# Forgetting attention in a 27,525-instruction transformer kernel: gate rows folded into the score matmul, a bf16 mask, heads in pairs in a fixed order

## The chip, the cores and the metric

The kernel runs on one core of one Trainium2 chip. The metric is the device time of one execution in microseconds (us). The core has five engines that work at the same time, each through its own queue in order: TensorE (PE; its weight loads are listed apart as PEld), VectorE (DVE), ScalarE (ACT), GpSimd (POOL) and SyncE (SP), which here only issues transfers. TensorE's clock is granted at one of two levels; the profile gives it as a share of full speed.

## The reference, cut to what matters

The program computes a mixture-of-experts block and then a block of two layers. Each of these has a token mixer, a cross attention and a feed-forward part. The change lies in the token mixer of the first layer, with 256 tokens, width 1024, 8 heads of 64 and 512 convolution channels:

```python
def forgetting_attention(q, k, v, log_f):
    cum = jnp.cumsum(log_f, axis=1).transpose(0, 2, 1)
    for blk in range(seq // 128):
        lo, hi = blk * 128, (blk + 1) * 128
        s = einsum("bqhd,bkhd->bhqk", q[:, lo:hi], k[:, :hi]) * scale
        s = s + cum[:, :, lo:hi, None] - cum[:, :, None, :hi]
        s = where(causal, s, NEG_INF)
        outs.append(einsum("bhqk,bkhd->bqhd", softmax(s), v[:, :hi]))

def fox_shortconv_mixer(h, w_in, b_f, conv_w, w_out):
    q, k, v, f_logit, b_gate, c_gate, u = split(h @ w_in)
    log_f = log_sigmoid(f_logit + b_f)
    y_a = forgetting_attention(heads(q), heads(k), heads(v), log_f)
    y_b = b_gate * causal_depthwise_conv(c_gate * u, conv_w)
    return concatenate([y_a, y_b]) @ w_out
```

## The kernel before, in words

The program is written as one long trace of operations. A planner puts them in order on each engine: it simulates the engines' time, and on each engine it takes the operation that is earliest in the text among those whose operands and buffers are ready. So work further down fills gaps, and the order in the queues is fixed before the run. `behind(marks)` adds an edge: what is traced in its block goes after the marked operation on the same engine.

Weights come as fp32 tiles through `colw` (256 columns) or `rows_load`, in a ring of three buffers, in the order of the text on SP. `wsp` splits a weight tile into a high part (ScalarE, L76) and the rest (VectorE, L77); a projection multiplies the split parts of weights and activations in three fp32r products (`mm3`, L85 to L87). Most split parts live in a ring of six pairs of buffers; where `wseq` holds an "F", a large buffer with the tag `f8` is used, which attention, recurrence and the prefetch of the next stage share. There are three `f8` buffers. `fgroup` makes one group of 128 output columns: 24 matmuls of 256 columns; `fmaj` makes two groups.

`fox` (L1255) is the token mixer. First come the values projection and the gate (8 rows), then the query and key projections (L1283 to L1285): each `fmaj` leaves two heads below each other in the partitions (0 to 63 and 64 to 127), and one ScalarE operation evacuates it into `qk`. The gate's logarithm and running sum are made on VectorE. `lq` and `rkx` (L1286 to L1302) hold the gate rows: for each head, 40 rows that give cum(query) - cum(key) as a product of their own.

`head` (L1304) does one head. For each of the two query tiles it issues three fp32 matmuls into one bank: query times key (L1310, 64 rows), the gate rows (L1312, 40 rows) and the identity times the causal mask `cm` (L1314). Then come two maxima (L1318, L1319), two exponentials with sums (L1320, L1321), the reciprocal and two scalings (L1322 to L1324), three transposes on TensorE (L1327), the copy into `pt` (L1329) and the products with the values: L1331 for the first key tile, L1332 for the second. The loop over `j` does two heads and one `split` into `ya`.

Behind the heads in the text, the loop of L1347 does the gated convolution in two halves: three projections each (`cproj`, two groups of 128 columns each, into the `acc` banks), the taps on VectorE (L1352 to L1355) and the gate product (L1356), split into `yb`. Last come the four output products with `out_pairs`: 24 matmuls of 512 columns for each of `yb[0]`, `yb[1]`, `ya[0]`, `ya[1]`. In the planned order the convolution groups stand between the steps of the heads. `boundary` then adds to the residual and makes the norm for the next stage. Ahead of `fox`, `first_norms` makes the first norm, with `rs_y` on GpSimd (L1051 to L1054).

Of the kernel before, what the change touches and what calls it, by code (L numbers as in the profile page):

```python
# [45 lines left out]
def block_kernel(ctx: ExitStack, tc: tile.TileContext, io, stop=None, dump=None):  # L46
# [897 lines left out]
    with ExitStack() as pctx:  # L944
# [10 lines left out]
        def wsp(w, a, b):  # L955
            pool = pq
            c = wseq.pop(0) if wseq else "W"
            if c == "F":
                pool = T(p0, [128, 2064], F32R, tag="f8", bufs=3)
            with behind(*marks.get(c, ())):  # L960
                return wsplit(pool, w, a, b, 6)

        def f8():
            return T(p0, [128, 2064], F32, tag="f8", bufs=3)

        def k8(t):
            return t[:, :2048].rearrange("p (a b) -> p a b", a=8)
# [114 lines left out]
                    prenorm_t(t, gn, *hl, rstd2(sx))  # L1082
            return hl

        def fgroup(ps, w, f, hl):
            wH, wL = wsp(w[:, :, f * 128 : (f + 1) * 128], KT, 128)
            po = ps.rearrange("p (t c) -> p t c", t=2)
            for k in range(KT):
                mm3(po, wH[:, k], wL[:, k], hl[0][:, :, k], hl[1][:, :, k], k == 0, k == KT - 1)

        def fmaj(w, hl, tag="sm", ps=None):
            if ps is None:
# [161 lines left out]

        def fox(h, pre):  # L1255
            w = io["ab_w_in_2"][0]
            qk = k8(f8())
            vc = f8()
            vt = vc[:, :1024].rearrange("p (t c) -> p t c", t=2)
            ct = vc[:, 1024:2048].rearrange("p (t c) -> p t c", t=4)  # L1260
# [13 lines left out]
            for k in range(KT):  # L1274
# [5 lines left out]
            G.memset(cm, 0.0)  # L1280
            G.affine_select(out=cm, in_=cm, pattern=[[-1, 128]], compare_op=ALU.is_ge, fill=NEG, base=0,
                            channel_multiplier=1)
            for c in range(2):  # L1283
                A.activation(qk[:, 2 * c : 2 * c + 2], fmaj(colw(w, c * 256), h), AF.Copy, scale=0.125)
                A.copy(qk[:, 4 + 2 * c : 6 + 2 * c], fmaj(colw(w, 512 + c * 256), h))  # L1285
            lq = T(pq, [104, S])  # L1286
            with behind(*marks["B"]):
                V.memset(lq[:64], 0.0)
                V.memset(lq[32:40], 1.0)
                rkx = tok()[:104].rearrange("p (a b) -> p a b", a=4)  # L1290
                V.memset(rkx, 0.0)
                one = wk_()[:8]
                V.memset(one, 1.0)
                oneh = [ident[0:8, b:8:2].unsqueeze(2).to_broadcast([8, 4, S]) for b in range(2)]
                log_sigmoid(pq, fz, fz, 8, S, "wk")
                V.tensor_tensor_scan(lq[0:8], one, fz, 0.0, ALU.mult, ALU.add)
                V.tensor_scalar(fz, lq[0:8], -1.0, None, ALU.mult)
                V.tensor_copy(lq[64:104], lq[0:40])
                for b in range(2):
                    A.copy(rkx[64 * b : 64 * b + 8], oneh[b])  # L1300
                    V.tensor_tensor(rkx[64 * b + 32 : 64 * b + 40], fz.unsqueeze(1).to_broadcast([8, 4, S]), oneh[b],
                                    ALU.mult)  # L1302

            def head(hd, po):  # L1304
                j, b0 = hd // 2, 64 * (hd % 2)
                ps = bank("sm")
                for t in range(2):
                    c0, n = (0, 128) if t == 0 else (128, 256)
                    tq = slice(t * 128, (t + 1) * 128)
                    PE.matmul(ps[:, c0 : c0 + n], qk[b0 : b0 + 64, j, tq], qk[b0 : b0 + 64, 4 + j, 0:n],  # L1310
                              start=True, stop=False)
                    PE.matmul(ps[:, c0 : c0 + n], lq[b0 : b0 + 40, tq], rkx[b0 : b0 + 40, j, 0:n],  # L1312
                              start=False, stop=False)
                    PE.matmul(ps[:, c0 + n - 128 : c0 + n], ident, cm, start=False, stop=True)  # L1314
                mx = T(pq, [128, 2], tag="mx", bufs=4)
                sm = T(pq, [128, 2], tag="smx", bufs=4)
                pr = T(pq, [128, 512], tag="pr", bufs=2)
                V.tensor_reduce(mx[:, 0:1], ps[:, 0:128], axis=AX.X, op=ALU.max, negate=True)  # L1318
                V.tensor_reduce(mx[:, 1:2], ps[:, 128:384], axis=AX.X, op=ALU.max, negate=True)  # L1319
                A.activation(pr[:, 0:128], ps[:, 0:128], AF.Exp, bias=mx[:, 0:1], accum_out=sm[:, 0:1])  # L1320
                A.activation(pr[:, 128:384], ps[:, 128:384], AF.Exp, bias=mx[:, 1:2], accum_out=sm[:, 1:2])  # L1321
                V.reciprocal(sm, sm)  # L1322
                V.tensor_scalar(pr[:, 0:128], pr[:, 0:128], sm[:, 0:1], None, ALU.mult)
                V.tensor_scalar(pr[:, 128:384], pr[:, 128:384], sm[:, 1:2], None, ALU.mult)  # L1324
                pst = bank("sm")
                for i in range(3):
                    PE.transpose(pst[:, i * 128 : (i + 1) * 128], pr[:, i * 128 : (i + 1) * 128], ident)  # L1327
                pt = T(pq, [128, 512], tag="pt", bufs=2)
                V.tensor_copy(pt[:, :384], pst[:, :384])  # L1329
                vs = slice(hd * 64, (hd + 1) * 64)  # L1330
                PE.matmul(po[b0 : b0 + 64, 0:256], vt[:, 0, vs], pt[:, 0:256], start=True, stop=False)  # L1331
                PE.matmul(po[b0 : b0 + 64, 128:256], vt[:, 1, vs], pt[:, 256:384], start=False, stop=True)  # L1332

            ya = [y2(), y2()]
            for j in range(4):
                po = bank("sm")
                head(2 * j, po)
                head(2 * j + 1, po)
                y = ya[j // 2]
                split(po[:, :256], y[0][:, j % 2], y[1][:, j % 2])  # L1340
            V.memset(cu[:, :, 0:2], 0.0)
            yb = []

            def cproj(c0):
                return fmaj(colw(w, c0), h, ps=accb())

            for c in range(2):  # L1347
                fs = slice(c * 2, c * 2 + 2)
                A.copy(ct[:, fs], cproj(2056 + c * 256))
                V.tensor_tensor(cu[:, fs, 2 : S + 2], cproj(2568 + c * 256), ct[:, fs], ALU.mult)  # L1350
                for f in (c * 2, c * 2 + 1):
                    V.tensor_scalar(cv[:, f], cu[:, f, 0:S], pcol("abcw", f), None, ALU.mult)  # L1352
                    for i in (1, 2):
                        V.scalar_tensor_tensor(cv[:, f], cu[:, f, i : i + S], pcol("abcw", i * 4 + f), cv[:, f],
                                               ALU.mult, ALU.add)  # L1355
                V.tensor_tensor(cv[:, fs], cproj(1544 + c * 256), cv[:, fs], ALU.mult)  # L1356
                y = y2()
                A.copy(y[0], cv[:, fs])
                V.tensor_tensor(y[1], cv[:, fs], y[0].bitcast(F32), ALU.subtract)
                yb.append(y)  # L1360
            acc = acc4()
            wo = io["ab_w_out_2"][0]
            out_pairs(acc, wo, [(2, yb[0])], True, False)
            out_pairs(acc, wo, [(3, yb[1])], False, False)
            out_pairs(acc, wo, [(0, ya[0]), (1, ya[1])], False, True)
            return acc

        def lru(h, pre):
# [167 lines left out]
```

## Time and profile before

| | us |
|---|---|
| median of 3 runs | 2400.92 (2395.62 to 2401.7) |
| the profiled execution, whole | 2400.16 |
| its span, first to last instruction | 2398.4 |
| TensorE busy | 2091.6 (87% of the span) |
| VectorE / ScalarE / GpSimd busy | 707.2 / 536.2 / 129.7 |

The first two thirds of the span are the expert layer, where the transfers run at some 400 GB/s. The two-layer block begins at about 1620 us. Its attention stage, from the first scores to the last output product, lies between 1673 and 1770 us. Times in the rows below are from the start of the span. In a timeline, a start is followed by a duration; matmuls are pipelined, so the distance between two starts is what one costs in a row of them. An fp32 matmul shows as two records. "[x <-engine tile line]" is idle time before an instruction and what ended it.

### The profile page before, as it was taken

The numbers are of one execution on the slowest core, as the hardware profiler recorded it, in microseconds if no ns is written. First come the engines' busy times: TensorE is split into PE (matmuls) and PEld (weight loads), VectorE is DVE, ScalarE is ACT, GpSimd is POOL, SyncE is SP. The second block draws the span as 40 slices with busy tenths as digits, with TensorE's granted clock in tenths as the row PEclk, the third lists the DMA queues.
The fourth block names the chain that finished last, engine by engine and source line by source line (L and its number), as shares of the span: only waits on it lengthen the run. The fifth ranks groups of instructions, "written<-read, shape, count | busy, mean of one in ns | idle before, by whom it ended". The sixth has DMA issues, their size and how long they took to land. (4 is left out here: it accounts for less than half of the span.)

```text
span 2398.4 us, 27525 instructions
## 1 busy us (share of the span) xinstructions
PE 2091.6 (87%) x11665; PEld 1258.9 (52%) x11665; DVE 707.2 (29%) x1237; ACT 536.2 (22%) x918; POOL 129.7 (5%) x205
## 2 busy tenths in 40 slices
PE   8998998779879879879877778778999999989998
PEld 7876432224423324423322222227777998977998
DVE  7674011000000000000000000007555545775544
ACT  5533000100000000000000000005354434764442
POOL 1521120000000000000000000002000000000000
PEclk9999999999999999999999999999999999999999
DMA  8327799999999999999999999997333655553653
GB/s 261 91 69 287 296 409 408 407 406 408 405 406 408 405 407 408 405 407 408 405 408 408 407 407 409 407 383 236 113 128 110 205 191 175 170 177 102 210 178 106
DMA packets 267803, 721.56 MB, mean 301 GB/s; under 512 B 7824, under 2 KB 102544, under 8 KB 267680
## 3 DMA queue, kind: packets, MB, share of 16 engines
q1 hardware_dynamic: 267376, 719.65, 79.1%
q8 instruction: 92, 1.51, 0.3%
q14 instruction: 31, 0.25, 0.0%
q10 hardware_dynamic: 304, 0.14, 0.0%
HBM read 718.72 MB, written 1.05 MB: 300 GB/s over the span
## 5 line engine op out<-in xcount | busy, mean ns | idle before, releaser
L768 PE MATMUL mm<-w,t 128*64 128x512 f32 (+3 forms) x1536 | 638.0, 566 | 135.3 <-DMA w<-in_w_up_dram 77.1
L769 PE MATMUL mm<-w,t 128*34 128x512 f32 (+1 forms) x1536 | 636.4, 565 | 0.0
L768 PEld LDWEIGHTS mm<-w,t 128*64 128x64 f32 (+1 forms) x1536 | 200.8, 137 | 324.1 <-issue 120.3
L795 PE MATMUL pj<-w,hT 128*34 128x512 f32 x1376 | 312.4, 597 | 51.7 <-DMA w<-in_w_down_dram 36.3
L779 DVE TENSOR_TENSOR hh<-sl,mm 98x512 f32<-98x512 f32 (+3 forms) x50 | 32.1, 642 | 1098.9 <-PE mm L769 1098.8
L769 PEld LDWEIGHTS mm<-w,t 128*34 128x34 f32 x1536 | 163.8, 113 | 222.7 <-issue 221.9
L77 DVE TENSOR_TENSOR wl<-w,wh 128x1024 fp32r<-128x1024 f32 (+1 forms) x196 | 232.7, 1207 | 159.9 <-ACT wh L76 154.5
L76 ACT CAST wh<-w 128x1024 fp32r<-128x1024 f32 (+1 forms) x196 | 197.5, 1032 | 230.9 <-DMA w<-in_w_ffn_gu_dram 64.4
L795 PEld LDWEIGHTS pj<-w,hT 128*34 128x34 f32 x1376 | 81.3, 112 | 245.8 <-issue 221.9
L776 ACT ACTIVATE sl<-mm 98x512 f32<-98x512 f32 (+3 forms) x50 | 28.0, 560 | 763.2 <-PE mm L769 759.4
L85 PE MATMUL sm<-hH,wh 128*128 128x256 f32 (+1 forms) x520 | 146.7, 282 | 0.0
L87 PE MATMUL sm<-hH,wl 128*128 128x256 f32 (+1 forms) x520 | 146.5, 282 | 0.0
L86 PE MATMUL sm<-hL,wh 128*128 128x256 f32 (+1 forms) x520 | 146.3, 281 | 0.0
L85 PEld LDWEIGHTS sm<-hH,wh 128*128 128x128 f32 (+1 forms) x520 | 97.2, 187 | 0.7
L86 PEld LDWEIGHTS sm<-hL,wh 128*128 128x128 f32 (+1 forms) x520 | 97.2, 187 | 0.7
L87 PEld LDWEIGHTS sm<-hH,wl 128*128 128x128 f32 (+1 forms) x520 | 97.1, 187 | 0.3
L77 DVE TENSOR_TENSOR f<-w,f 128x1024 fp32r<-128x1024 f32 x71 | 84.8, 1220 | 30.4 <-ACT f L76 30.4
L85 PE MATMUL acc<-wh,yH 128*128 128x512 f32 x192 | 78.8, 410 | 5.6 <-ACT yH L1445 4.5
L76 ACT CAST f<-w 128x1024 fp32r<-128x1024 f32 x71 | 72.3, 1047 | 32.6 <-PE acc L87 13.6
L85 PE MATMUL pj<-uyH,wh 128*128 128x272 f32 x256 | 77.2, 303 | 1.2 <-ACT qT L314 1.2
L86 PE MATMUL acc<-wl,yH 128*128 128x512 f32 x192 | 78.1, 407 | 0.0
L87 PE MATMUL pj<-uyH,wl 128*128 128x272 f32 x256 | 75.7, 296 | 0.0
(468 smaller groups left out, 2974.9 us busy)
## 6 DMA issues: line engine op xcount, KB each, us to landing
w<-in_w_gate_dram SPq DMA_DIRECT2D x64, 2048.0 KB, 23.6
w<-in_w_up_dram SPq DMA_DIRECT2D x64, 2048.0 KB, 23.9
w<-in_w_down_dram SPq DMA_DIRECT2D x64, 2048.0 KB, 24.0
w<-in_w_down_dram SPq DMA_DIRECT2D x30, 1536.0 KB, 18.9
w<-in_w_ffn_gu_dram SPq DMA_DIRECT2D x44, 1024.0 KB, 5.6
w<-in_w_gate_dram SPq DMA_DIRECT2D x16, 1920.0 KB, 24.0
w<-in_w_up_dram SPq DMA_DIRECT2D x16, 1920.0 KB, 19.9
w<-in_w_ffn_down_dram SPq DMA_DIRECT2D x22, 1024.0 KB, 6.1
```

The source lines that it names most:

```text
L76: A.copy(hv, w)
L77: V.tensor_tensor(lv, w, hv.bitcast(F32), ALU.subtract)
L85: PE.matmul(ps, lh, rh, start=first, stop=False)
L86: PE.matmul(ps, lh, rl, start=False, stop=False)
L87: return PE.matmul(ps, ll, rh, start=False, stop=last)
L768: PE.matmul(ps[:m, :hw], xs[:, k, e * CAP : e * CAP + m], w[k][:, :hw], start=st, stop=sp)
L769: PE.matmul(ps[64 : 64 + CAP, :hw], xs[:, k, es], w[k][:, hw:], start=st, stop=sp)
L776: A.activation(sl[r, :hw], pg[r, :hw], AF.Silu)
L779: V.tensor_tensor(hh[r, :hw], sl[r, :hw], pu[r, :hw], ALU.mult)
L795: PE.matmul(dn[64 * c : 64 * c + CAP], hT_[:, j * CAP : (j + 1) * CAP], d[j][:, c * 512 : (c + 1) * 512], start=f == 0, stop=f == DFF // 1 ...
```

## The change

Query rows (0 to 63), gate rows (64 to 71 and 96 to 103) and zero rows between them stand in one tile for all heads, `qh`, and the same for keys, `kh`; both are `f8` buffers. A head's score of one query tile is then one matmul over 104 rows. The constant rows are filled on GpSimd, as is a one-hot pattern that picks each head's gate row. The evacuation of the projections is by half the partitions (four ScalarE operations for the queries, two on ScalarE and two on VectorE for the keys). The mask is put into the bank first, by one bf16 matmul of 384 columns (`idb`, `cmb`). The `f8` ring has four buffers in place of three.

`head` is taken apart into `scores`, `soft`, `turn` and `values`, and the convolution into twelve `pieces`, each one group of 128 columns. The loop over pairs issues them in a fixed order: scores of two heads, two pieces, transposes of two heads, one piece, values of two heads. `mk` holds the last TensorE instruction of each step, and the next step goes behind it. The value products of the two heads alternate. The output products come in the order `yb[0]`, `ya[0]`, then `yb[1]` and `ya[1]` together.

```diff
-                pool = T(p0, [128, 2064], F32R, tag="f8", bufs=3)
+                pool = T(p0, [128, 2064], F32R, tag="f8", bufs=4)
...
-            return T(p0, [128, 2064], F32, tag="f8", bufs=3)
+            return T(p0, [128, 2064], F32, tag="f8", bufs=4)
...
-            qk = k8(f8())
+            qh, kh = k8(f8()), k8(f8())
...
+            cmb, idb = T(pq, [128, 384], BF16), T(pq, [128, 128], BF16)
+            G.memset(cmb, 0.0)
+            G.tensor_copy(cmb[:, 0:128], cm)
+            G.tensor_copy(cmb[:, 256:384], cm)
+            G.tensor_copy(idb, ident)
+            oneh = ident[0:8, 0:8].unsqueeze(2).to_broadcast([8, 8, S])
+            G.memset(qh[64:96], 0.0)
+            G.memset(qh[96:104], 1.0)
+            G.memset(kh[64:104], 0.0)
+            G.tensor_copy(kh[64:72], oneh)
             for c in range(2):
-                A.activation(qk[:, 2 * c : 2 * c + 2], fmaj(colw(w, c * 256), h), AF.Copy, scale=0.125)
-                A.copy(qk[:, 4 + 2 * c : 6 + 2 * c], fmaj(colw(w, 512 + c * 256), h))
+                pq_ = fmaj(colw(w, c * 256), h)
+                for b in range(2):
+                    A.activation(qh[0:64, 4 * c + b : 4 * c + 4 : 2], pq_[64 * b : 64 * b + 64], AF.Copy, scale=0.125)
+                pk_ = fmaj(colw(w, 512 + c * 256), h)
+                A.copy(kh[0:64, 4 * c : 4 * c + 4 : 2], pk_[0:64])
+                last = V.tensor_copy(kh[0:64, 4 * c + 1 : 4 * c + 4 : 2], pk_[64:128])
...
-                V.tensor_copy(lq[64:104], lq[0:40])
-                for b in range(2):
-                    A.copy(rkx[64 * b : 64 * b + 8], oneh[b])
-                    V.tensor_tensor(rkx[64 * b + 32 : 64 * b + 40], fz.unsqueeze(1).to_broadcast([8, 4, S]), oneh[b],
-                                    ALU.mult)
+                for c in range(2):
+                    hs = slice(4 * c, 4 * c + 4)
+                    A.copy(qh[64:72, hs], fc.unsqueeze(1).to_broadcast([8, 4, S]))
+                    V.tensor_tensor(kh[96:104, hs], fz.unsqueeze(1).to_broadcast([8, 4, S]), oneh[:, hs], ALU.mult)
...
+            def cproj(c0, use):
+                wt, ps = colw(w, c0), accb()
+                for f in range(2):
+                    def piece(f=f):
+                        sp = wsp(wt[:, :, f * 128 : (f + 1) * 128], KT, 128)
+                        with behind(*mk):
+                            m = fgroup(ps[:, f * 256 : (f + 1) * 256], wt, f, h, sp)
+                        mk[:] = [m]
+                        if f:
+                            use(two(ps))
+                    pieces.append(piece)
...
+            def scores(hd):
                 ps = bank("sm")
-                for t in range(2):
-                    c0, n = (0, 128) if t == 0 else (128, 256)
-                    tq = slice(t * 128, (t + 1) * 128)
-                    PE.matmul(ps[:, c0 : c0 + n], qk[b0 : b0 + 64, j, tq], qk[b0 : b0 + 64, 4 + j, 0:n],
-                              start=True, stop=False)
-                    PE.matmul(ps[:, c0 : c0 + n], lq[b0 : b0 + 40, tq], rkx[b0 : b0 + 40, j, 0:n],
-                              start=False, stop=False)
-                    PE.matmul(ps[:, c0 + n - 128 : c0 + n], ident, cm, start=False, stop=True)
+                with behind(*mk):
+                    PE.matmul(ps[:, :384], idb, cmb, start=True, stop=False)
+                    for t, c0, n in ((0, 0, 128), (1, 128, 256)):
+                        m = PE.matmul(ps[:, c0 : c0 + n], qh[0:104, hd, t * 128 : (t + 1) * 128], kh[0:104, hd, 0:n],
+                                      start=False, stop=t == 1)
+                mk[:] = [m]
+                return ps
...
+            def values(j, pts):
                 po = bank("sm")
-                head(2 * j, po)
-                head(2 * j + 1, po)
+                with behind(*mk):
+                    for t, (o, i0, i1) in enumerate(((0, 0, 256), (128, 256, 384))):
+                        for b in range(2):
+                            vs = slice((2 * j + b) * 64, (2 * j + b + 1) * 64)
+                            m = PE.matmul(po[64 * b : 64 * b + 64, o:256], vt[:, t, vs], pts[b][:, i0:i1],
+                                          start=t == 0, stop=t == 1)
+                mk[:] = [m]
...
+            for j in range(4):
+                pss = [scores(2 * j + b) for b in range(2)]
+                prs = [soft(ps) for ps in pss]
+                for i in range(2):
+                    pieces.pop(0)()
+                pts = [turn(pr) for pr in prs]
+                pieces.pop(0)()
+                values(j, pts)
             acc = acc4()
             wo = io["ab_w_out_2"][0]
             out_pairs(acc, wo, [(2, yb[0])], True, False)
-            out_pairs(acc, wo, [(3, yb[1])], False, False)
-            out_pairs(acc, wo, [(0, ya[0]), (1, ya[1])], False, True)
+            out_pairs(acc, wo, [(0, ya[0])], False, False)
+            out_pairs(acc, wo, [(3, yb[1]), (1, ya[1])], False, True)
```

## Rows read from the trace of the kernel before

**Rows 1.** Stretches: length; busy PE, PEld, DVE, ACT, POOL; PE clock; DMA share, GB/s.

```profile
1676.00:1726.70 50.70, 50.03 (x365) 44.52 (x363) 29.40 (x59) 18.55 (x36) 0.00 (x0) 1.00 0.39 125
1726.70:1744.00 17.30, 13.82 (x46) 9.21 (x47) 7.72 (x18) 4.30 (x13) 0.00 (x0) 0.71 0.18 61
1744.00:1770.00 26.00, 25.50 (x112) 19.13 (x111) 11.12 (x17) 9.83 (x20) 1.43 (x4) 1.00 0.37 122
```

**Rows 2.** The same for TensorE alone: length, busy, clock, DMA share, GB/s.

```profile
1732.90:1744.10 11.20, 10.30 (x30) 0.54 0.00 0
```

**Rows 3.** TensorE's waits, 1673 to 1770: us in total, times, longest.

```profile
PE sm L1327 <- DVE pr L1323: 2.3, 1, 2.3
PE sm L1331 <- DVE pt L1329: 1.7, 2, 0.9
```

**Rows 4.** Timeline of TensorE: one head's values, the next head's scores, split products.

```profile
1706.79 0.65 PE L1331 MATMUL sm<-pt,f 128*64 128x256 f32 x2
1707.27 0.38 PE L1332 MATMUL sm<-pt,f 128*64 128x128 f32 x2
1707.58 0.49 PE L1310 MATMUL sm<-f 64*128 64x128 f32 x2
1707.91 0.38 PE L1312 MATMUL sm<-tok,t 40*128 40x128 f32 x2
1708.22 0.49 PE L1314 MATMUL sm<-t,t 128*128 128x128 f32 x2
1708.64 0.70 PE L1310 MATMUL sm<-f 64*128 64x256 f32 x2
1709.17 0.59 PE L1312 MATMUL sm<-tok,t 40*128 40x256 f32 x2
1709.70 0.49 PE L1314 MATMUL sm<-t,t 128*128 128x128 f32 x2
1709.94 0.36 PE L86 MATMUL acc<-hL,wh 128*128 128x256 f32 x1
1710.14 0.29 PE L87 MATMUL acc<-hH,wl 128*128 128x256 f32 x1
1710.26 0.28 PE L85 MATMUL acc<-hH,wh 128*128 128x256 f32 x1
```

**Rows 5.** Timeline of TensorE in the expert layer: products for two halves of the partitions.

```profile
1524.26 0.49 PE L768 MATMUL mm<-w,t 128*64 128x384 f32 x1
1524.27 0.49 PE L769 MATMUL mm<-w,t 128*34 128x384 f32 x1
1524.58 0.49 PE L768 MATMUL mm<-w,t 128*64 128x384 f32 x1
```

**Rows 6.** Timeline of VectorE: first reduction and last scaling of two heads.

```profile
1710.22 0.29 DVE L1318 TENSOR_REDUCE mx<-sm 128x1 f32<-128x128 f32 x1 [1.21 <-PE sm L1314]
...
1712.29 0.35 DVE L1324 TENSOR_SCALAR pr<-pr,smx 128x256 f32<-128x256 f32 x1
...
1718.23 0.29 DVE L1318 TENSOR_REDUCE mx<-sm 128x1 f32<-128x128 f32 x1 [1.75 <-PE sm L1314]
...
1723.63 0.34 DVE L1324 TENSOR_SCALAR pr<-pr,smx 128x256 f32<-128x256 f32 x1
```

**Rows 7.** GpSimd, groups by line and form: a fill (busy us, mean ns).

```profile
L833 POOL MEMSET ysb<- 128x1024 f32 x2 | 1.8, 952 | 39.3 <-PE mm L707 39.3
```

**Rows 8.** ScalarE, groups by line and form, 1615 to 1770: query evacuation.

```profile
L1284 ACT ACTIVATE f<-sm 128x512 f32<-128x512 f32 x2 | 1.2, 589 | 0.0
```

**Rows 9.** Timelines: end of the gate rows, first scores, last output product.

```profile
1667.65 2.46 DVE L1301 TENSOR_TENSOR tok<-t,t 8x1024 f32<-8x1024 f32 x2
...
1673.09 0.49 PE L1310 MATMUL sm<-f 64*128 64x128 f32 x2
...
1769.58 0.40 PE L87 MATMUL acc<-wh,yL 128*128 128x512 f32 x1
```

## What the change does to the time: the prediction, made before the run

> **What bounds the kernel now.** I read the stretches first: they tell which engine sets the pace of the attention stage and where it loses it. From 1676 to 1726.7 us TensorE is busy 50.03 of 50.70 us at a granted clock of 1.00, while VectorE is busy 29.4 and ScalarE 18.6: the stage is bound by TensorE, and whatever is taken out of its queue there ends the stage earlier. Between 1726.7 and 1744 us it is busy only 13.82 of 17.30 at a mean clock of 0.71, and from 1744 on it is full again [rows 1]. So there is a hole 17 us long. Its second part, 1732.9 to 1744.1, runs at 0.54, which is mostly the lower of the two levels, 1.2 GHz [rows 2]. The list of TensorE's waits names what opened it: the transposes of L1327 wait for the normalised rows of L1323 (2.3 us, once) and the value products of L1331 for the copy of L1329 (1.7 us in two) [rows 3]. That is one head's chain from scores to softmax to transposes to values with nothing left to put beside it: by 1726 all twelve convolution groups have been used as filler, and the last three heads run almost alone. Last I read the timeline of one head for the price of each matmul [rows 4].
>
> **Scores, on the path.** A head now issues six fp32 matmuls: L1310, L1312 and L1314 for each of the two query tiles. From the first (1707.58) to the first matmul of other work (1709.94) that is 2.36 us [rows 4]. The starts in between show the parts: the 128-column ones are 0.31 to 0.42 apart, the 256-column ones 0.53. After the change a head has three: one bf16 matmul of 384 columns with the mask, and the two score products with 104 rows, which hold query, key and gate rows together. The row count does not show in the price: 64 rows (1708.64 to 1709.17) and 40 rows (1709.17 to 1709.70) both take 0.53 for 256 columns, so I take 0.33 and 0.53 for the new ones. No bf16 matmul stands in this trace. Nearest is the split product with fp32r operands, 256 columns in 0.12 us (1710.14 to 1710.26) [rows 4], which makes 0.18 for 384. The other end is the fp32 rate: 128 more columns cost 0.53 - 0.33 = 0.20, so 384 cost about 0.75. I take 0.24, near the fp32r row because bf16 is no wider than fp32r, with a little for the change of operands. New sum 0.24 + 0.33 + 0.53 = 1.10; saved 2.36 - 1.10 = 1.26 per head, 8 x 1.26 = 10.1 us. Ends: 6.0 (mask at 0.75) and 11.7 (mask 0.18, and products at 0.72 together because the switches between 40 and 128 rows are gone).
>
> **Values, on the path.** Each head issues L1331 and L1332, 0.48 + 0.31 = 0.79 us [rows 4]. The number of instructions stays, but the order changes: for each key tile the products of head 2j go to partitions 0 to 63 and those of head 2j+1 to 64 to 127, one right behind the other. The expert layer does just this in L768 and L769: two products for different halves of the partitions start 0.01 us apart, and the next pair stands 0.32 behind for 384 columns of one pass [rows 5]; they run side by side. So a pair should take 0.79 in place of 1.58: 4 x 0.79 = 3.2 us. Ends: 0 and 3.2. The Trainium skill says the same in "TensorE: Matmul & The Clock Gate", Part 3 (packing small matmuls): outputs that start in different column groups run concurrently. By that rule the sum below stands; without it, it would be 3.2 us smaller.
>
> **The hole, on the path.** The new order lays two convolution groups between a pair's scores and its transposes, and a third between transposes and values; `mk` chains them on TensorE. Twelve groups, three per pair, so the last pair has its fillers too. Then the two waits, 4.0 us [rows 3], go, and with them the low clock: 10.30 us of work at 0.54 would take 10.30 x 0.54 = 5.6 us at full clock, which gives back 4.7 [rows 2]. Together 8.7. What is late next: behind the last values stand the output products of `yb[0]` and `ya[0]`, whose operands are long ready, so the split of `ya[1]` and the gate product of `yb[1]` lie beside them.
>
> **What the fixed order costs.** A chained TensorE can no longer take other convolution work when a softmax is late. The cover is two groups of 24 matmuls, 48 x 0.12 = 5.8 us. From the first reduction to the end of the normalisation a head needs 2.4 us where VectorE is free (1710.22 to 1712.64), and 5.7 where weight splits and convolution taps stand between (1718.23 to 1723.97) [rows 6]. So the second head of a pair is ready 0.3 + 2.4 to 0.3 + 5.7 us after its scores, against 5.8. Behind the transposes there is one group, 2.9 us, for two copies. I take 0.5 us a pair, 2 in all; ends 0 and 10 (2.5 a pair, when two slow softmaxes meet on one VectorE). Queued behind a waiting transpose are the third group, the values and the next scores: the whole chain waits.
>
> **What lies beside other work.** GpSimd gets three fills and one copy of 2048 columns and four small operations: at 0.95 us for 1024 columns [rows 7] some 1.9 each, about 8 us, and under 2 for the small ones. Ahead of the gate rows it has all of the first projections; its cover is gone only if the fills are queued in front of the `rs_y` operations of the first norm, on which the first transposes wait: 0 to 1.9 us (one fill), and I take 0. ScalarE gets two more evacuations of 0.59 (L1284) [rows 8], VectorE two of about that and loses four fills and a copy. Both have slack in the query and key projections, where TensorE runs without a gap. The gate rows: the products of L1301 end at 1670.1 and the first scores start at 1673.09 [rows 9], 3 us of slack; the two ScalarE copies, so far made early, now follow the scan, but only the first is needed for the first four heads. No load moves: the order of the transfers on SP stays, and the heads issue none. The fourth `f8` buffer shifts the pool behind it by 8 KB, so other transfers wait for other buffers of the expert layer, and later weight splits find one more free buffer. The trace shows no price; I bound it by the longest single TensorE wait of the stage, 2.3 us [rows 3], to either side, and take 1 us of loss.
>
> **Sum.** 10.1 + 3.2 + 8.7 - 2 - 1 = 19.0 us. The profiled execution took 2400.16 us, of which the span is 2398.4; 2400.16 - 19.0 = 2381.2. The median of the runs is 0.8 above that execution, so 2382.
>
> **Rivals.** (a) The hole stays, at another place: the last values, their split and the output weights come too late, or the planner lets the filler run out. For it speaks that this happened to the kernel before; against it the fixed count of fillers. Only scores and values are gained: 13.3 - 1 to 3; time about 2390. (b) Slower: the softmax of a pair does not fit under its two groups, since VectorE takes splits and convolution taps first, and TensorE idles in each of the four pairs long enough to lose its clock. Its price per pair is that of the old hole, 4.0 idle, and 4.7 of low clock, 35 in all; less the 22 gained (10.1 + 3.2 + 8.7) the kernel ends at about 2414. It decides from 5.5 us a pair. For it speaks the 5.7 us softmax, against it that all four pairs must then be as slow, and that a wait of 0.3 to 2.5 us is shorter than the two that cost the clock here, 4.0 together. The Trainium skill, in "TensorE: Matmul & The Clock Gate" (Why this matters for your kernels), warns of idle gaps between bursts of matmuls because the clock falls to half; rows 2 agree, 0.54 behind the waits. (c) The new forms do not pay: the mask at the fp32 rate, values one behind the other, stalls of 2.5 us a pair. 6.0 + 0 + 8.7 - 10 - 1 = 3.7 us; 2397, within the noise. (d) More than forecast: no stalls, all the upper ends, and the spare buffer helps later stages: 11.7 + 3.2 + 8.7 + 2.3 = 25.9; 2375 or below.
>
> **How the numbers follow.** Forecast (2376 to 2388) 0.57; (a) 0.19; (b) 0.09; (c) 0.09; (d) 0.06. A measurement of this kernel can tell about 0.3%, 7 us, from no change. Faster by more: forecast, (a), (d) and a small part of (c), 0.83; within 0.3%: most of (c), 0.08; slower: (b), 0.09. The range leaves out (b) and the far ends of (c) and (d): 2375 to 2397.
>
> **What would show it.** Right: between the end of the key projection and the boundary TensorE at clock 1.00 with under 3 us idle; from a head's mask matmul to its last score about 1.1 us; value products of two heads starting within 0.02 us of each other; the stage ending near 1750 in place of 1770 [rows 9]. Wrong: waits of the transposes for the normalised rows in each pair, a stretch at 0.5, bf16 matmuls of 0.6 us or more, or a first norm that waits for GpSimd.

## The result, and the profile after

The changed kernel takes 2368.89 us (median of 4 runs, 2362.77 to 2369.3); the kernel before took 2398.36 in the same comparison (4 runs, 2395.62 to 2401.7). The ratio is 0.9864, with a 95% interval of 0.985 to 0.9877: faster, by 29 us, which is 13 us below the forecast of 2382 and below its range. The profiled execution took 2369.3 us (span 2367.5), 30.9 less than the 2400.16 of the profiled execution before. All sums below are between these two executions.

First the stretches of the attention stage of the changed kernel: length, busy time of PE, PEld, DVE, ACT and POOL with instruction counts, granted TensorE clock, DMA share, GB/s.

```profile
1673.00:1700.00 27.00, 27.00 (x221) 25.52 (x220) 22.86 (x50) 13.93 (x33) 0.00 (x0) 1.00 0.52 164
1700.00:1727.00 27.00, 27.00 (x195) 23.90 (x194) 19.72 (x38) 13.45 (x26) 0.00 (x0) 1.00 0.47 163
1727.00:1744.00 17.00, 16.41 (x73) 12.93 (x71) 9.93 (x11) 8.26 (x17) 1.93 (x5) 1.00 0.49 165
```

TensorE is busy in every microsecond but the last 0.6, at a clock of 1.00. The hole of [rows 1] and the 0.54 of [rows 2] are gone. TensorE's waits from 1660 to 1760 (total, times, longest) hold nothing of the stage any more; what is left belongs to the boundary behind it:

```profile
PE acc L1106 <- DVE hL L82: 0.9, 2, 0.5
PE sm L1025 <- DVE tok L1021: 0.6, 1, 0.6
```

The two waits of [rows 3] have no successor. Now TensorE's timeline around one pair's scores, around the first pair's values, and at the end of the stage (start, duration, engine, line, tiles, shapes):

```profile
1672.88 0.34 PE L1349 MATMUL sm<-t,t 128*128 128x384 bf16 x1
1673.05 0.82 PE L1351 MATMUL sm<-f,f 104*128 104x128 f32 x4
1673.71 0.33 PE L1349 MATMUL sm<-t,t 128*128 128x384 bf16 x1
1673.87 0.82 PE L1351 MATMUL sm<-f,f 104*128 104x128 f32 x4
1674.34 0.47 PE L85 MATMUL acc<-hH,wh 128*128 128x256 f32 x1
...
1683.75 0.87 PE L1385 MATMUL sm<-pt,f 128*64 128x256 f32 x8
1684.56 0.34 PE L1349 MATMUL sm<-t,t 128*128 128x384 bf16 x1
...
1742.55 0.40 PE L87 MATMUL acc<-wh,yL 128*128 128x512 f32 x1
1743.54 0.44 PE L1025 MATMUL sm<-t,tok 128*128 128x128 f32 x2 [0.58 <-DVE tok L1021]
```

The first head of the pair, with the second behind it, takes 1673.71 - 1672.88 = 0.83 us from mask to mask. The second, with a convolution group behind it, takes 1674.34 - 1673.71 = 0.63: there the next matmul's start comes 0.2 us sooner. Over all eight heads it is 5.85 / 8 = 0.73, where [rows 4] show 2.36. A pair's values take 1684.56 - 1683.75 = 0.81, where one head alone took 0.79. The first scores start as before, at 1672.88 against 1673.09 in [rows 9], and the stage ends 27 us sooner, at 1742.78 in place of 1769.81.

I counted each matmul from its own start to the start of the next, waits taken out, from the first score to the last output product:

| us | before | after | difference |
|---|---|---|---|
| scores | 20.87 | 5.85 | -15.0 |
| transposes of the softmax | 4.12 | 2.13 | -2.0 |
| values | 7.11 | 3.79 | -3.3 |
| convolution groups | 35.63 | 35.26 | -0.4 |
| output products | 24.52 | 22.87 | -1.65 |
| waits | 4.47 | 0.0 | -4.5 |
| stage | 96.72 | 69.90 | -26.8 |

The other 4.1 us lie outside. The two feed-forward stages take 192.68 and 191.83 in place of 195.20 and 194.23, -4.9 together; the stretches ahead of the scores and behind the output products are 1.6 shorter; the expert layer ends 0.7 later (in the profiles of this study its end moves between 1625 and 1633); and the recurrent stage is 1.9 longer. For the last of these TensorE's waits in that stage give the place (before from 2036 to 2132, after from 2005 to 2103). Before:

```profile
PE sm L1025 <- DVE tok L1021: 0.7, 1, 0.7
```

After:

```profile
PE sm L1025 <- DVE tok L1021: 2.4, 1, 2.4
```

The boundary's transposes wait 2.4 us for the normalised tokens in place of 0.7. ScalarE's timeline shows what came in between. Before, the sum of squares of the new residual (L1003) starts as soon as VectorE has it:

```profile
2126.29 0.63 ACT L1003 ACTIVATE junk<-hx 128x512 bf16<-128x512 f32 x1 [1.92 <-DVE hx L1076]
```

After, the split of an output weight of the cross attention into an `f8` buffer stands ahead of it in ScalarE's queue, and waits for its transfer:

```profile
2097.03 1.05 ACT L76 CAST f<-w 128x1024 fp32r<-128x1024 f32 x1 [2.62 <-DMA w<-in_w_xo_dram]
2097.98 0.63 ACT L1003 ACTIVATE junk<-hx 128x512 bf16<-128x512 f32 x1
```

From the start of L1076 to that of L1003 it is 2.49 us (2095.49 to 2097.98) in place of 0.84 (2125.45 to 2126.29). The kernel before makes this split only behind the boundary (2144.56); the kernel with the fourth buffer alone, below, has it in the same place as here, where it waits 1.18 us. So the spare buffer brings the split forward, and what that costs depends on when its transfer lands.

### The profile page after: what moved, and what is told of

Read it like the earlier page. It is cut to its first block, busy times and chain, and to the rows that moved or that the text cites. A ratio compares the mean times of both kernels' runs of the same rounds, so it can differ in the third digit from the quotient of the medians.

```text
span 2367.5 us, 27434 instructions
## 1 busy us (share of the span) xinstructions
PE 2065.2 (87%) x11609; PEld 1240.0 (52%) x11609; DVE 709.1 (30%) x1235; ACT 538.9 (23%) x920; POOL 139.2 (6%) x213
## 5 line engine op out<-in xcount | busy, mean ns | idle before, releaser
L77 DVE TENSOR_TENSOR wl<-w,wh 128x1024 fp32r<-128x1024 f32 (+1 forms) x196 | 234.8, 1216 | 137.2 <-ACT wh L76 130.8
L86 PE MATMUL sm<-hL,wh 128*128 128x256 f32 (+1 forms) x520 | 144.6, 278 | 0.0
L77 DVE TENSOR_TENSOR f<-w,f 128x1024 fp32r<-128x1024 f32 x71 | 85.7, 1222 | 48.7 <-ACT f L76 48.7
L86 PEld LDWEIGHTS sm<-hL,wh 128*128 128x128 f32 (+1 forms) x520 | 96.8, 186 | 0.7
L86 PE MATMUL acc<-wl,yH 128*128 128x512 f32 x192 | 77.1, 401 | 0.0
```

The source lines that it names most:

```text
L77: V.tensor_tensor(lv, w, hv.bitcast(F32), ALU.subtract)
L86: PE.matmul(ps, lh, rl, start=False, stop=False)
```

## The experiments

**The fourth buffer alone.** The kernel before with four `f8` buffers and nothing else:

```
-                pool = T(p0, [128, 2064], F32R, tag="f8", bufs=3)
+                pool = T(p0, [128, 2064], F32R, tag="f8", bufs=4)
...
-            return T(p0, [128, 2064], F32, tag="f8", bufs=3)
+            return T(p0, [128, 2064], F32, tag="f8", bufs=4)
```

> The kernel before, with four f8 buffers in place of three and nothing else changed. Theory 1: the spare buffer is what shortened the two feed-forward stages of the changed kernel (195.2 to 192.7 us and 200.5 to 198.1 us); then those two stages lose about 2.5 us each here too, the attention stage stays at 96.7 us with its hole, and the kernel is about 3 to 5 us faster (2396 against 2400). Rival: those 5 us come from another order that the planner found once the attention stage had changed; then this kernel is within 1 us of before and both feed-forward stages are as before.

Measured: 2394.87 us, ratio 0.9978 (0.9967 to 0.9988), 5 us faster. The attention stage is as it was (96.18). The feed-forward stages take 192.84 and 191.69, as in the changed kernel. In the first of them TensorE's waits before were these:

```profile
...
PE sm L1025 <- DVE tok L1021: 1.0, 2, 0.6
PE acc L86 <- DVE f L77: 0.9, 1, 0.9
...
```

and with four buffers these:

```profile
PE acc L1105 <- ACT hH L81: 1.5, 1, 1.5
PE sm L1025 <- DVE tok L1021: 1.0, 2, 0.6
...
```

The wait for a weight split held in an `f8` buffer (`f`, L77) has gone. It explains 0.9 of the 2.4 us. Most of the rest is no listed wait but spread over the stage: its 960 split products of 256 columns take 112.9 us from start to start in place of 114.1. Why is open. The gain belongs to the buffer and not to the attention stage.

**The new form in the old order of text, without the chain.** The heads have the mask, the 104-row products and their tiles as in the change; the text goes from one head's scores through its softmax to its transposes, then to the next head and the pair's values, the convolution groups follow all heads, the output products have their old order, and `mk` stays empty:

```
-                pss = [scores(2 * j + b) for b in range(2)]
-                prs = [soft(ps) for ps in pss]
-                for i in range(2):
-                    pieces.pop(0)()
-                pts = [turn(pr) for pr in prs]
-                pieces.pop(0)()
+                pts = [turn(soft(scores(2 * j + b))) for b in range(2)]
                 values(j, pts)
+            while pieces:
+                pieces.pop(0)()
```

> The changed kernel with the new score form, but in the order of the kernel before: no chain on TensorE, heads one after the other in the text, convolution groups behind them, output products in the old order. Theory 1: the form alone gives what the scores measured, 8 x (2.36 - 0.73) = 13.0 us, and 3.3 us at the values, while the hole at the end of the heads stays with some 4.5 us of waits and as much of low clock; the attention stage takes about 80 us and the kernel about 2380. Rival: once the scores are short, more of a head's time is softmax, the planner uses up its filler at the same point, and the hole grows by what the scores gave: stage 85 us or more, kernel 2385 or more.

Measured: 2370.86 us, ratio 0.9885 (0.9867 to 0.9904); the stage takes 74.16. Scores 5.46, values 5.55, waits 1.83. Both expectations missed, for the planner filled nearly all of the hole by itself. What is left of the waits is this pair of lines in TensorE's timeline (idle time before the instruction and its releaser in brackets):

```profile
1714.18 0.86 PE L1382 MATMUL sm<-pt,f 128*64 128x256 f32 x6 [1.54 <-DVE pt L1373]
1715.34 0.30 PE L1371 MATMUL sm<-t,pr 128*128 128x128 f32 x1 [0.29 <-DVE pr L1363]
```

So the form alone takes 22.0 of the 26.3 us by which the changed kernel's stage is shorter than that with four buffers (96.18).

**The order alone.** The fixed order and the chain of the change, with a head's six old score matmuls:

```
+            def scores(hd):
+                ps = bank("sm")
+                with behind(*mk):
+                    j, b0 = hd // 2, 64 * (hd % 2)
+                    for t in range(2):
...
+                        PE.matmul(ps[:, c0 : c0 + n], lq[b0 : b0 + 40, tq], rkx[b0 : b0 + 40, j, 0:n],
+                                  start=False, stop=False)
+                        m = PE.matmul(ps[:, c0 + n - 128 : c0 + n], ident, cm, start=False, stop=True)
+                mk[:] = [m]
```

> The changed kernel with its fixed order, value order and four buffers, but with the old scores: six fp32 matmuls a head, gate rows and fp32 mask as products of their own. Theory 1: the hole is gone and the scores cost 2.36 us a head again: attention stage 69.9 + 8 x 1.63 = 83 us, no waits, kernel about 2382. Rival: part of the 15 us that the score lines lost was low clock and not form; then the scores here take less than 2.2 us a head and the kernel is at 2378 or below.

Measured: 2381.68 us, ratio 0.9932 (0.9915 to 0.9948); stage 89.47, waits 0.0, values 3.76. The stage is 6 us longer than the 83 of the first theory, and the surprise is why. TensorE alone, one microsecond a row (length, busy with count, granted clock, DMA share, GB/s), from the first pair of scores, which begins at 1667.98:

```profile
1668.00:1669.00 1.00, 1.00 (x7) 1.00 0.55 62
...
1670.00:1671.00 1.00, 1.00 (x7) 1.00 1.09 389
1671.00:1672.00 1.00, 1.00 (x5) 0.68 1.10 362
1672.00:1673.00 1.00, 1.00 (x3) 0.50 1.01 314
...
1677.00:1678.00 1.00, 1.00 (x7) 0.50 0.00 0
1678.00:1679.00 1.00, 1.00 (x10) 0.90 0.00 0
1679.00:1680.00 1.00, 1.00 (x11) 1.00 0.00 0
```

and its timeline over the fall:

```profile
1667.98 0.49 PE L1346 MATMUL sm<-f 64*128 64x128 f32 x2
...
1669.04 0.70 PE L1346 MATMUL sm<-f 64*128 64x256 f32 x2
1669.57 0.59 PE L1348 MATMUL sm<-tok,t 40*128 40x256 f32 x2
...
1671.71 1.22 PE L1346 MATMUL sm<-f 64*128 64x256 f32 x2
1672.73 1.05 PE L1348 MATMUL sm<-tok,t 40*128 40x256 f32 x2
```

TensorE has work in every row and waits for nothing, and still the clock goes to 0.50, the 1.2 GHz level, 3 us after the old scores of two heads began. The same matmul of 256 columns takes 0.53 to its successor at 1669.04 and 1.02 at 1671.71. The clock returns at 1678 to 1679, among convolution groups. The clock falls again with the third and the fourth pair, and not with the second. Transfers don't decide it: none runs where the last of these falls comes (the last two figures of the row), and a kernel below keeps 1.00 beside busier queues.

```profile
1722.00:1723.00 1.00, 1.00 (x6) 0.78 0.00 0
```

Over all three falls the scores take 21.27 in place of 8 x 2.36 = 18.9, and the convolution groups 39.35 in place of 35.26: together the 6 us. So a pair of old scores in one go can lower the clock without a wait; it did so in three pairs of four.

**The row count.** The changed kernel, its 104-row products each as 96 rows and the 8 rows of the key gates:

```
-                        m = PE.matmul(ps[:, c0 : c0 + n], qh[0:104, hd, t * 128 : (t + 1) * 128], kh[0:104, hd, 0:n],
-                                      start=False, stop=t == 1)
+                        for r in (slice(0, 96), slice(96, 104)):
+                            m = PE.matmul(ps[:, c0 : c0 + n], qh[r, hd, t * 128 : (t + 1) * 128], kh[r, hd, 0:n],
+                                          start=False, stop=t == 1 and r.stop == 104)
```

> The changed kernel with each 104-row score product taken apart into one of 96 rows and one of 8 rows (partitions 96 to 103), same result. Theory 1: a switch between whole-array products and products on a few partitions costs time of its own, which is why the old scores cost 2.36 us and not the 1.1 + 0.8 us that columns alone explain; then a head's scores go from 0.73 us to more than 1.38, by 0.1 us or more for each of four switches: about 1.8 us a head, 8 to 9 us in all. Rival: only columns count: 0.73 + 0.22 + 0.43 = 1.38 us a head, 5.2 us in all.

Measured: 2381.78 us, ratio 0.9935 (0.9917 to 0.9954); scores 17.25, so 2.16 a head in place of 0.73. The first head's timeline:

```profile
1673.97 0.34 PE L1349 MATMUL sm<-t,t 128*128 128x384 bf16 x1
1674.14 2.05 PE L1352 MATMUL sm<-f,f 96*128 96x128 f32 x8
1676.13 0.34 PE L1349 MATMUL sm<-t,t 128*128 128x384 bf16 x1
```

and the weight loads beside it (the bracket is time in which the loads waited for nothing that the profile names):

```profile
1673.97 1.20 PEld L1352 LDWEIGHTS sm<-f,f 96*128 96x128 f32 x6
1675.50 0.29 PEld L1352 LDWEIGHTS sm<-f,f 8*128 8x128 f32 x2 [0.33 <-issue]
1676.12 0.10 PEld L1349 LDWEIGHTS <-t 128*128 128x128 bf16 x1 [0.33 <-issue]
```

Two more products a head, of 128 and 256 columns, should add 0.65 us by their columns (the whole 0.66 of L1351 above). They add 1.43. The other 0.78 go with the four changes between the whole array and 8 rows, about 0.2 each, and at two of them the loads stand still for 0.33. The Trainium skill, in "TensorEngine Tiling (Array Packing)", Key Properties, says that a change of the tiling mode drains TensorE. The pauses agree with that; no run shows in which mode the 8-row products ran.

**Count and width without the small rows.** As many fp32 products as the old heads had and as wide, but all on 104 or 128 rows: each score product twice, and the mask in fp32 for each query tile. The doubled product makes the scores twice as large, so its output is another:

```
-                    PE.matmul(ps[:, :384], idb, cmb, start=True, stop=False)
...
+                        for i in range(2):
+                            PE.matmul(ps[:, c0 : c0 + n], qh[0:104, hd, t * 128 : (t + 1) * 128], kh[0:104, hd, 0:n],
+                                      start=i == 0, stop=False)
+                        m = PE.matmul(ps[:, c0 + n - 128 : c0 + n], ident, cm, start=False, stop=True)
```

> The changed kernel with as many and as wide score products as the old form, six fp32 products a head, but all over the whole array: each 104-row product is issued twice (so the scores come out doubled, which changes the result) and the mask is one fp32 product of 128 columns for each query tile. Theory 1: the old form's price above its columns, and its low clock, came from products on 64 and 40 rows and the switches to and from them; then a head costs its columns alone, 4 x 0.22 + 2 x 0.44 = 1.76 us, 3.5 us a pair, the granted clock stays at 1.00 through the heads, and the stage takes 69.9 + 8 x 1.03 = 78 us. Rival: six fp32 products in a row are dear in any shape and let the clock fall; then a head takes 2.2 us or more, a stretch behind a pair shows a clock under 1.00, and the stage takes 85 us or more.

Measured: 2375.49 us (one run); stage 77.77, scores 14.04, 1.76 a head. One head, from 1673.24 to 1675.00:

```profile
1673.24 0.61 PE L1351 MATMUL sm<-f,f 104*128 104x128 f32 x4
1673.68 0.39 PE L1353 MATMUL sm<-t,t 128*128 128x128 f32 x2
1673.91 1.03 PE L1351 MATMUL sm<-f,f 104*128 104x256 f32 x4
1674.77 0.39 PE L1353 MATMUL sm<-t,t 128*128 128x128 f32 x2
1675.00 0.61 PE L1351 MATMUL sm<-f,f 104*128 104x128 f32 x4
```

A product of 128 columns costs 0.22 and one of 256 costs 0.43. TensorE over a stretch with these scores:

```profile
1660.00:1680.00 20.00, 20.00 (x171) 1.00 0.71 215
```

The clock holds, here and in the three stretches of 20 us behind it. With the same number and width, two things are missing: the 0.6 us a head (2.36 - 1.76) and the fall of the clock. Both belong to the products on 64 and 40 rows with their changes. In the kernel with 96 and 8 rows, which has four such changes a head, the clock falls once, behind the third pair, again with no wait of TensorE in the stage:

```profile
1708.00:1711.00 3.00, 3.00 (x16) 0.50 0.23 93
```

So products on 64 and 40 rows aren't needed for it. Which of the two, few rows or the changes, lowers the clock isn't settled.

**The mask in fp32.** The changed kernel with `cmb` and `idb` in fp32:

```
-            cmb, idb = T(pq, [128, 384], BF16), T(pq, [128, 128], BF16)
+            cmb, idb = T(pq, [128, 384]), T(pq, [128, 128])
```

> The changed kernel with the mask product of 384 columns in fp32 in place of bf16. Theory 1: fp32 costs by columns, two records of 384 columns, 0.64 us for 0.17, so 0.5 us more a head, 4 us in all (stage 74 us), and no fall of the clock, because the product covers the whole array like its neighbours. Rival: the old scores were dear because they were fp32 and came in a row of six, and their long runs alone let the clock fall; then here, too, a stretch shows a granted clock under 1.00 and the stage is over 76 us.

Measured: stage 74.11, scores 9.98 in place of 5.85. The kernel's 2369.05 us (one run) say little, because its expert layer ended 4 us earlier.

```profile
1669.98 0.81 PE L1349 MATMUL sm<-t,t 128*128 128x384 f32 x2
1670.63 0.82 PE L1351 MATMUL sm<-f,f 104*128 104x128 f32 x4
```

The mask costs 0.65 in fp32 and 0.17 in bf16 (1672.88 to 1673.05 above): 4.1 us for eight heads, and the clock stays. This is the price of the type alone, as expected.

**Values head by head.** The changed kernel with the two loops of `values` exchanged:

```
-                    for t, (o, i0, i1) in enumerate(((0, 0, 256), (128, 256, 384))):
-                        for b in range(2):
+                    for b in range(2):
+                        for t, (o, i0, i1) in enumerate(((0, 0, 256), (128, 256, 384))):
```

> The changed kernel with the value products of a pair one head after the other, as before, in place of alternating. Theory 1: alternating products for the two halves of the partitions run side by side and that is all the gain at the values: 0.8 us a pair becomes 1.6, stage 69.9 + 3.2 = 73.1 us. Rival: the gain came from making the two heads' products in one go, without a switch to other work in between; then the pair stays under 1.2 us and the stage under 71.5.

Measured: 2368.87 us (one run), stage 70.03, values 4.03 in place of 3.79.

```profile
1682.81 0.88 PE L1385 MATMUL sm<-pt,f 128*64 128x256 f32 x8
1683.62 0.34 PE L1349 MATMUL sm<-t,t 128*128 128x384 bf16 x1
```

Still 0.81 for a pair. Products for the two halves of the partitions run side by side in either order, as long as both heads' stand together in the queue. Where they stood apart, in the kernel with the form alone and the one without the chain, the sum was 5.5.

**Without the chain.** The changed kernel with the four lines `mk[:] = [m]` taken out, so that the planner orders TensorE's work:

> The changed kernel without the chain on TensorE: text order of pairs and groups as in the change, but the planner may take other work. Theory 1: with short scores the planner fills nearly as well by itself: stage 70 to 72 us, waits under 1 us, kernel within 0.2% of the changed one. Rival: the chain is what keeps fillers for the last pair; then waits of 2 us or more come back near the end of the heads and the stage is 74 us or more, as in the form alone (74.2).

Measured: 2368.58 us, ratio 0.9873 (0.9856 to 0.989), no other than with the chain. The stage takes 72.23, 2.3 more (values 5.49, scores 6.44), waits 0.0. What the chain holds together is worth 2.3 us of the stage, which can't be told apart in the kernel's time.

**Without the groups between.** The chain kept, but the three convolution groups of a pair behind its values:

```
-                for i in range(2):
-                    pieces.pop(0)()
                 pts = [turn(pr) for pr in prs]
-                pieces.pop(0)()
                 values(j, pts)
+                for i in range(3):
+                    pieces.pop(0)()
```

> The changed kernel with no convolution group between a pair's scores and its transposes nor between transposes and values; the three groups follow the values. The chain holds, so TensorE must wait for each softmax. Theory 1: four waits of 3.5 to 5 us for the softmax and four of about 1 us for the copies, 18 to 24 us in all, stage 88 to 94 us at a clock that stays at 1.00, because each wait stands alone between three groups. Rival (the prediction's slower case): each wait takes the clock down with it, some 4.7 us more a pair, stage over 100 us and the kernel at 2400 or above.

Measured: 2389.43 us, ratio 0.9953 (0.9938 to 0.9969); stage 91.67. TensorE waits 11.9 us in eight waits, which are two for each pair:

```profile
1672.41 0.61 PE L1373 MATMUL sm<-t,pr 128*128 128x128 f32 x3 [3.00 <-DVE pr L1365]
1673.55 0.61 PE L1373 MATMUL sm<-t,pr 128*128 128x128 f32 x3 [0.53 <-DVE pr L1365]
```

and its clock falls in every stretch that holds a pair:

```profile
1660.00:1680.00 20.00, 16.45 (x118) 0.91 0.51 158
1680.00:1700.00 20.00, 17.31 (x124) 0.91 0.16 53
```

The two stretches behind these show 0.91 as well: one fall for each pair. Of the 21.8 us over the changed kernel 11.9 are waits. At 0.91 over 20 us the lower clock takes 1.8 us a pair at most, some 7 of the other 9.9. The rest isn't clock: the transposes cost 4.99 in place of 2.13, and the first pair's stand ahead of its fall; a product with a wait behind it is counted to its end and not to the next start. So with the new form the clock falls behind waits, and a pair without cover costs 5.4 us. The first theory's stage of 88 to 94 us was met; its 18 to 24 us of waits and its clock of 1.00 were not.

**A fifth buffer.** Since the fourth helped, a fifth, paid for by one pair of the buffers for weight splits (6 to 5):

```
-                pool = T(p0, [128, 2064], F32R, tag="f8", bufs=4)
+                pool = T(p0, [128, 2064], F32R, tag="f8", bufs=5)
...
-                return wsplit(pool, w, a, b, 6)
+                return wsplit(pool, w, a, b, 5)
```

> The changed kernel with a fifth f8 buffer, paid for with one of the six pairs of small split buffers. Theory 1: the fourth buffer took away the waits of the feed-forward stages' first products for late splits, and a fifth finds nothing more to take; within 0.2% of the changed kernel, feed-forward stages 192 to 193 us. Rival: more large buffers let the next stage's weights come still earlier, and each feed-forward stage loses another microsecond or more.

Measured: 2377.31 us, ratio 0.9915 (0.9894 to 0.9935), slower than the change. The feed-forward stages are at 195.63 and 194.11 again and the second cross stage at 70.77 (68.07). Two things changed at once, so whether the missing pair or the fifth buffer itself costs the time isn't shown; together they lose the gain of the fourth, which neither theory had. No kernel tried is faster than the change by more than a measurement tells.

## Why the prediction was right or wrong

The prediction had 19.0 us, the two executions differ by 30.9. Its mechanism held: TensorE bounds the stage, what leaves its queue comes off the end, and the hole closes. The direction is right, and inside the stage every gain came; the cost of the fixed order did not. The missing 11.9 us are 5.1 outside the stage and 6.8 inside, by the steps:

**The spare buffer: wrong sign, the first step that failed.** I took 1 us of loss, because "the trace shows no price", and named a gain only in rival (d). The buffer brings 5 us, shown by the kernel that has nothing else. [rows 3] were the wrong rows to bound it by: they are of the attention stage, and the place to look was the list of waits of the stages that draw on `f8`, where `PE acc L86 <- DVE f L77` stood in both feed-forward stages. Even that row, 0.9 us each, would have given 1.8 of the 4.9. A loss came too, in the recurrent stage: the split brought forward by the buffer makes the boundary's transposes wait 1.7 us longer. Outside the stage the forecast was +1 and the outcome -4.1.

**Scores: mis-sized, the second step that failed.** Forecast 1.10 a head, measured 0.73: 3.0 us for eight. The mask came at 0.17 instead of 0.24, the end of the range that goes by the fp32r rate of [rows 4]. The products together cost 0.66 instead of 0.86; the last 0.1 is the sooner start of the group behind every second head. What failed is "the row count does not show in the price": in [rows 4] each of the first five start-to-start distances, from which I took my prices, held a change of rows as well. Against 0.22 and 0.43 for products that follow others of the whole array, the old distances are 0.33, 0.31, 0.42, 0.53 and 0.53: each change cost 0.1 to 0.2, 0.6 a head. I had put this into the upper end (0.72 together), where the trace already spoke for it: the 0.24 of the last L1314 before the split products was a 128-column product without a change behind it, beside 0.42 for the same line with one.

**Values: right size, other reason.** 3.3 us against 3.2. The new order within a pair isn't what makes them run side by side; that the two heads' products are neighbours is.

**The hole: right in sum, its cause half told.** The waits went (4.5 against 4.0). One reading was off: only two of the last three heads ran almost alone, the last head's scores stand among the output products, at 1748.26. The table's remaining gains, which are 2.0 of the scores beyond 8 x (2.36 - 0.73) = 13.0, and 2.0, 1.65 and 0.4 on transposes, output products and convolution, make 6.0, where I had 4.7 for the low clock. [rows 1] bound the clock's part: 17.30 x (1 - 0.71) = 5.0 us at most; the rest isn't parted. I named the waits as the cause of the 0.54 in [rows 2]. The experiments show a fall from either: behind waits with the new form (0.91 over 20 us), and in the old scores without any wait (0.50). Which did it before can't be told, since there both came together. The rule that I cited from the Trainium skill, "TensorE: Matmul & The Clock Gate" (Why this matters for your kernels), that idle gaps between bursts of matmuls lower the clock, agrees with the kernel without groups; the kernel with the order alone goes beyond it, since its clock fell with no gap.

**The fixed order: 0 instead of 2 us.** Not one wait is left in the stage, so 5.8 us of groups did cover both softmaxes. The 5.7 of [rows 6] was a softmax on a VectorE that had splits and taps in its way; in the kernel without groups a pair's softmax held the first transposes up for 3.0 us at most.

**Beside other work: right.** GpSimd's fills and the copies cost nothing that I can find: the first norm begins at 1630.77 against 1630.03, the expert layer having ended as much later, and the first scores start no later. VectorE lost three fills, not four.

**The rivals.** (a) fell: no wait is left. (b)'s mechanism is real, but its premise isn't met: with the groups away a pair loses 5.4 us, just under the 5.5 from which it was to decide, and the kernel still stays 0.5% faster than before. The scores gained more than it had set against that price. (c) fell in all its parts: the mask isn't at the fp32 rate (0.17 against 0.65), values run side by side, and nothing stalls. (d) had the right terms (no stalls, upper ends, buffer), at 25.9 us; its own buffer term, 2.3, was half of what came.

Of form and order, which the prediction added up as if they were apart, the form is nearly everything: 22.0 us of the stage alone, the order 6.7 alone, 26.3 together. In the kernel with the form alone the twelve groups are used up at 1710.6, with two heads' scores still to come in place of three, and no large hole is left.

## What to carry to other kernels

Price a matmul from a place where its neighbours use the array in the same way: a distance between starts on both sides of a change of row count holds the change too, and joining rows into one wide contraction saved that here, more than the columns tell. Before putting a stall down to its last wait, look whether the clock had reason to fall without one, and try the short form of the work before writing an order by hand. When a pool gets another buffer, read the waits of every stage that draws on it, not those of the stage being edited.

## What the runs showed of the hardware

- The granted clock fell to 0.50 while TensorE was busy in every microsecond, during a run of fp32 products on 64, 40 and 128 rows, in three pairs of heads of four; the first time it came back 7 us later. With products on 96 and 8 rows it fell once, with products of the old number and width on 104 and 128 rows it stayed at 1.00.
- A change between products on many and on few rows cost 0.1 to 0.2 us on TensorE (old scores; 96 and 8 rows), and the weight loads paused 0.33 us at two such places.
- Start to start at full clock and without such a change: fp32 0.22 us for 128 columns, 0.43 for 256, 0.65 for 384; bf16 0.17 for 384.
- Value products for partitions 0 to 63 and 64 to 127 overlapped (0.81 us for two heads, 0.79 for one) when issued head by head too.
